# The FFN input products of a hybrid encoder by seven quarter products of fp32r pairs instead of eight

## The chip, the cores and the metric

The kernel runs on one core of one Trainium2 chip. The metric is the time of one execution on the device in microseconds (us). The engines are TensorE (PE in the profile, its weight loads PEld), VectorE (DVE), ScalarE (ACT), GpSimd (POOL) and SyncE (SP), which issues the DMAs.

## What is computed

Two layers of an encoder trunk on 512 tokens with 1024 features, in fp32:

```python
for i in range(DEPTH):                                   # DEPTH = 2
    h = h + 0.5 * swiglu_ffn(rms_norm(h, ffn1_norm[i]), ffn1_w_in[i], ffn1_w_out[i])
    u = rms_norm(h, mix_norm[i])
    z, xbc, dt_raw, q_a, kv_a, k_rope_raw = split_in_proj(u @ w_in_mix[i])
    y_ssd = ssd_mixer(...)                               # a chunked scan
    y_mla = mla_mixer(...)                               # latent attention, 8 heads
    h = h + jnp.concatenate([y_ssd, y_mla], axis=-1) @ w_out_mix[i]
    h = h + 0.5 * swiglu_ffn(rms_norm(h, ffn2_norm[i]), ffn2_w_in[i], ffn2_w_out[i])
    h = h + jax.nn.sigmoid(rms_norm(h, ple_norm[i]) @ w_ple_gate[i]) * (p[i] @ w_ple_proj[i])
return rms_norm(h, final_norm)

def swiglu_ffn(x, w_in, w_out):                          # w_in (1024, 5632), w_out (2816, 1024)
    g, u = jnp.split(x @ w_in, 2, axis=-1)
    return (jax.nn.silu(g) * u) @ w_out
```

There are four such FFNs, two in each layer. The change concerns the product `x @ w_in` in each of them.

## The kernel before

Activations lie transposed: features in the 128 partitions, the 512 tokens in the free dimension, so `h` is 8 tiles of 128x512. An fp32 product is made from three matmuls of fp32r, a type with a shorter mantissa: each operand is split into `hi`, its rounding to fp32r, and `lo`, the rest, and the product is hi x hi + hi x lo + lo x hi (`acc_wx`, lines 344 to 346), added up in a PSUM bank of 128x512.

Weights are planned as a list of units in the order in which the products take them. A unit is a tile `raw` of 128x1024 that one DMA loads (line 226); ScalarE rounds it to `hi` (L240) and VectorE subtracts to get `lo` (L241). `weights(key)` hands out the next unit and keeps the loads five units and the splits two units ahead (LOOK_DMA, LOOK_SPLIT); there are four raw tiles and three of `hi` and of `lo`.

An FFN (`ffn`) goes over 22 feature tiles f. For each, the gate's and the up-projection's product run over 8 tiles of the contraction, 24 matmuls of 512 columns each, into two banks. Then `evac` multiplies the gate by the token's norm factor `rb` (DVE, L465), applies SiLU (ACT, L467), multiplies by the up-projection (DVE, L468) and splits the result into `hi` and `lo` (`halves`, L357 on ACT and L358 on DVE). The output product then takes these 22 pairs as operands for each of 8 output tiles (66 matmuls each, with three weight units); the result is scaled (L500), added to `h` (L502), and the next norm gets the tile.

The norm's gain is multiplied into the operand while it is split (`add_operand`: ACT L382, DVE L383, two instructions of 512 columns for each of 8 tiles); the squares go into an accumulator (L404, L405), and the factor per token comes from it later (`stats`, `spread`).

The second FFN of a layer follows the mixer, whose last part adds the attention's output product to `h` tile by tile (L1088); the first FFN of the second layer follows the per-layer input (`ple`). In attention, `scores` makes the softmax rows of one block of 128 queries in a buffer `pr`, and `flip` transposes them, up to three blocks later.

Each `S()` takes one of 74 buffers of 128x512 (NSLOT), each `B()` one of eight PSUM banks. Between engines the framework sets the waits; it also sets the order in which each engine's instructions are issued: by the order of the code where two are ready, but one that is not ready is passed by later ones.

Of the kernel before, what the change touches and what calls it, by code (L numbers as in the profile page):

```python
# [17 lines left out]
P = 128  # L18
# [21 lines left out]
NSLOT = 74  # L40
NRAW = 4
NW = 3
LOOK_DMA = 5
LOOK_SPLIT = 2

# 2*pi as a sum of pieces; the first two have 12 bits, so that 11 bits times them are exact
# [20 lines left out]
class _Slots:  # L67
    """Buffers of one size, each with a tag of its own, handed out in the order they came free."""
# [17 lines left out]
def kernel(ctx: ExitStack, tc: tile.TileContext, a: dict, out: bass.AP):  # L86
# [8 lines left out]
    p_raw = ctx.enter_context(tc.tile_pool(name="p_raw", bufs=NRAW))  # L95
    p_hi = ctx.enter_context(tc.tile_pool(name="p_hi", bufs=NW))
# [10 lines left out]

    def sm(tag, shape, dt=F32, bufs=None):
        uid[0] += 1
        return small.tile(list(shape), dt, tag=tag, name=f"{tag}_{uid[0]}", bufs=bufs)  # L110
# [8 lines left out]
    units = []  # L119

    def unit(key, nk, cols, *loads):
        units.append((key, nk, cols, loads))
# [82 lines left out]
    loaded, split = [], []  # L205
    later = deque()

    def load_one():
# [3 lines left out]
        key, nk, cols, loads = units[len(loaded)]  # L212
# [14 lines left out]
        loaded.append((raw, nk, cols))  # L227
# [3 lines left out]

    def split_one():
        j = len(split)
        while len(loaded) <= j:
            load_one()
        raw, nk, cols = loaded[j]
# [3 lines left out]
        A.copy(hi[:, :n], raw[:, :n])  # L240
        V.tensor_tensor(lo[:, :n], raw[:, :n], hi[:, :n].bitcast(F32), op=ALU.subtract)  # L241
        loaded[j] = None
# [5 lines left out]
    def weights(key):  # L248
# [3 lines left out]
        while len(loaded) < min(j + 1 + LOOK_DMA, len(units)):  # L252
            load_one()
        while len(split) < min(j + 1 + LOOK_SPLIT, len(units)):
            split_one()
# [51 lines left out]
    tri = const.tile([P, P], F32, name="tri")        # 1 where row <= column  # L307
    stri = const.tile([P, P], F32, name="stri")      # 1 where row > column
# [6 lines left out]
    mk_l = const.tile([P, P], BF16, name="mk_l")     # row 0: queries of the first chunk  # L315
    mk_r = const.tile([P, P], BF16, name="mk_r")     # row 0: keys of the second chunk
# [44 lines left out]
    class Norm:  # L361
        """RMS norm over the feature tiles added to it: the gain goes into the products'
        operand, the per-token factor is applied to what the products give."""
# [26 lines left out]
        def add_part(self, y, src, cs):  # L390
            """Some columns of the last tile."""
# [6 lines left out]
        def add_square(self, src):  # L398
# [3 lines left out]
            else:  # L402
                sq = S()
                A.activation(sq.ap, src, AF.Square)  # L404
                V.tensor_tensor(self.acc.ap, self.acc.ap, sq.ap, op=ALU.add)  # L405
                slots.put(sq)
# [45 lines left out]

    def gain(i, nm):
        return lambda k: vcol(i, nm, k)
# [4 lines left out]
    def ffn(i, nm, norm, nxt, start=lambda: None, tables=lambda: None):  # L459
        hid = []  # L460

        def evac(bg, bu):
            # the per-token factor of `u` is applied after the output product
            g = S()
            V.tensor_tensor(g.ap, bg.ap, norm.rb.ap, op=ALU.mult)  # L465
            banks.put(bg)
            A.activation(g.ap, g.ap, AF.Silu)  # L467
            V.tensor_tensor(g.ap, bu.ap, g.ap, op=ALU.mult)  # L468
            banks.put(bu)
            hi, lo = S(F32R), S(F32R)  # L470
            halves(g.ap, hi.ap, lo.ap)
            slots.put(g)
            hid.append((hi, lo))

        X = norm.ops
        held = []
        for f in range(KF):
            bg, bu = B(), B()
            acc_wx(bg.ap, weights((i, nm, "g", f)), X)
            if f == 0:  # L480
                start()
                norm.stats()
            if f == 2:
                norm.spread()
            acc_wx(bu.ap, weights((i, nm, "u", f)), X)
            held.append((bg, bu))
            if f >= 2:
                for pair in held:
                    evac(*pair)
                held = []  # L490
            if f == 4:
                tables()
        norm.drop(rb=False)
        H = [(p.ap, q.ap) for p, q in hid]
        for m in range(KD):
            b = B()
            for k0 in range(0, KF, 8):
                acc_wx(b.ap, weights((i, nm, "o", m, k0)), H, k0, k0 == 0, k0 + 8 >= KF)
            t = S()
            V.scalar_tensor_tensor(out=t.ap, in0=b.ap, scalar=0.5, in1=norm.rb.ap, op0=ALU.mult, op1=ALU.mult)  # L500
# [812 lines left out]
```

## Time and profile before

| | |
|---|---|
| median of 3 runs | 2345.74 us (2345.72 to 2346.37) |
| span of the profiled execution | 2343.0 us (its own run time is not listed beside it) |
| TensorE busy | 2330.0 us, 10950 matmuls |
| VectorE busy | 1245.1 us, 1944 instructions |
| ScalarE busy | 885.3 us, 1388 instructions |
| GpSimd busy | 126.0 us, 136 instructions |
| mean granted TensorE clock | 0.999 of full speed |
| DMA | 209.73 MB, 90 GB/s in the mean |

The span runs from the first to the last instruction of the program. A row of a group gives the line, engine and operation, the written and read buffers, the shape, the count, and behind the bar the busy time in us, the mean of one in ns, and the engine's idle time just before these instructions with what ended it. A row of the timeline gives start and duration in us.

### The profile page before, as it was taken

The page shows a single profiled execution, that of the slowest core. Times are in us where ns is not written, and L with a number is a line of the kernel's source. Part 1 is how long each engine was busy: PE and PEld are TensorE (multiplying, and loading weights), DVE is VectorE, ACT ScalarE, POOL GpSimd, SP SyncE. Part 2 cuts the span into 40 slices and gives each one's busy share as a digit, 9 for nine tenths or more (in the row PEclk, how much of TensorE's full clock was granted, in tenths as well). Part 3 has the DMA queues.
Part 4 walks back from the last instruction along what each step waited for, and adds up shares of the span by engine and source line. Part 5 has one row for each costly group of instructions (what it writes and reads, how often), then busy time and mean ns, then how long its engine had stood idle before and what let it go on. Part 6 is the DMA issues. An engine that isn't in the chain of part 4 may idle for free.

```text
span 2343.0 us, 27624 instructions
## 1 busy us (share of the span) xinstructions
PE 2330.0 (99%) x10950; PEld 1933.4 (83%) x10950; DVE 1245.1 (53%) x1944; ACT 885.3 (38%) x1388; POOL 126.0 (5%) x136
## 2 busy tenths in 40 slices
PE   9999999999999999999999999999999999999998
PEld 7888888888888888888888888888888888888887
DVE  5543345688676434434644443466876764443345
ACT  4322224455455322222432222244544543222224
POOL 0000000223000000000000000011320000000000
PEclk9999999999999999999999999999999999999999
DMA  5333333221222333332333333332112223333322
GB/s 159 97 99 98 91 96 102 88 61 43 75 81 72 100 99 99 92 95 88 100 103 99 92 95 99 95 101 82 49 53 64 93 74 106 96 94 95 99 75 84
DMA packets 396110, 209.73 MB, mean 90 GB/s; under 512 B 19438, under 2 KB 390348, under 8 KB 395980
## 3 DMA queue, kind: packets, MB, share of 16 engines
q1 hardware_dynamic: 395980, 207.96, 30.6%
q8 instruction: 86, 1.41, 0.3%
q14 instruction: 44, 0.36, 0.0%
HBM read 205.83 MB, written 2.10 MB: 89 GB/s over the span
## 4 chain that ended last, share of the span: by engine, by line
PE 99%; DMA 0%; SPq 0%; DVE 0%; ACT 0%; POOL 0%; issue 0%
PE b L344 28%; PE b L345 28%; PE b L346 28%; PE b L353 2%; PE b L352 2%; PE b L354 2%; PE b L852 1%; PE b L1017 1%; PE b L1043 0%; PE b L833 0%; PE b L836 0%; PE b L993 0%; PE b L990 0%; PE b L1044 0%; PE b L992 0%; PE b L991 0%
## 5 line engine op out<-in xcount | busy, mean ns | idle before, releaser
L344 PE MATMUL b<-s,hi 128*128 128x512 f32 (+2 forms) x2906 | 1139.1, 393 | 0.0
L346 PE MATMUL b<-s,lo 128*128 128x512 f32 (+2 forms) x2906 | 1131.2, 390 | 0.0
L345 PE MATMUL b<-s,hi 128*128 128x512 f32 (+2 forms) x2906 | 1130.9, 390 | 0.0
L240 ACT CAST hi<-raw 128x1024 fp32r<-128x1024 f32 (+3 forms) x428 | 412.1, 963 | 1121.7 <-PE b L345 656.2
L241 DVE TENSOR_TENSOR lo<-raw,hi 128x1024 fp32r<-128x1024 f32 (+3 forms) x428 | 480.6, 1124 | 349.7 <-ACT hi L240 338.7
L346 PEld LDWEIGHTS b<-s,lo 128*128 128x128 f32 (+1 forms) x2906 | 545.4, 188 | 113.4
L344 PEld LDWEIGHTS b<-s,hi 128*128 128x128 f32 (+1 forms) x2906 | 545.8, 188 | 112.6 <-issue 2.4
L345 PEld LDWEIGHTS b<-s,hi 128*128 128x128 f32 (+1 forms) x2906 | 545.7, 188 | 112.5 <-issue 2.9
L468 DVE TENSOR_TENSOR s<-b,s 128x512 f32<-128x512 f32 x88 | 60.5, 691 | 254.6 <-PE b L346 250.9
L465 DVE TENSOR_TENSOR s<-b,s 128x512 f32<-128x512 f32 x88 | 60.1, 690 | 202.3 <-PE b L346 202.3
L430 POOL TENSOR_TENSOR nr<-nv,half 128x4 f32<-128x4 f32 (+1 forms) x14 | 19.1, 1366 | 1759.9 <-DVE nv L422 1759.1
L357 ACT CAST s<-b 128x128 fp32r<-128x128 f32 (+2 forms) x196 | 66.8, 360 | 102.6 <-DVE s L358 34.0
L358 DVE TENSOR_TENSOR s<-b,s 128x128 fp32r<-128x128 f32 (+2 forms) x196 | 75.4, 402 | 33.2 <-ACT s L357 31.7
L352 PE MATMUL b<-hi,s 128*128 128x512 f32 (+1 forms) x208 | 77.9, 375 | 0.0
L353 PE MATMUL b<-hi,s 128*128 128x512 f32 (+1 forms) x208 | 77.2, 371 | 0.0
L354 PE MATMUL b<-lo,s 128*128 128x512 f32 (+1 forms) x208 | 76.2, 366 | 0.0
L358 DVE TENSOR_TENSOR s<-s,s 128x512 fp32r<-128x512 f32 x104 | 71.0, 685 | 1.1 <-ACT s L357 0.7
L357 ACT CAST s<-s 128x512 fp32r<-128x512 f32 x104 | 64.6, 622 | 5.6 <-DVE s L976 4.6
L382 ACT ACTIVATE s<-s,vec 128x512 fp32r<-128x512 f32 x56 | 40.4, 722 | 56.4 <-DVE s L502 46.7
L608 DVE SCALAR_TENSOR_TENSOR s<-s,vec,s 128x511 f32<-128x511 f32 (+2 forms) x72 | 60.8, 848 | 0.6
L500 DVE SCALAR_TENSOR_TENSOR s<-b,s 128x512 f32<-128x512 f32 x32 | 22.1, 692 | 65.4 <-PE b L346 65.4
L467 ACT ACTIVATE s<-s 128x512 f32<-128x512 f32 x88 | 54.8, 626 | 0.4
(221 smaller groups left out, 1612.9 us busy)
## 6 DMA issues: line engine op xcount, KB each, us to landing
raw<-in_ffn_w_in_dram SPq DMA_DIRECT2D x176, 512.0 KB
raw<-in_ffn_w_out_dram SPq DMA_DIRECT2D x64, 512.0 KB
raw<-in_w_in_mix_dram SPq DMA_DIRECT2D x50, 512.0 KB
raw<-in_w_out_mix_dram SPq DMA_DIRECT2D x32, 512.0 KB
raw<-in_ffn_w_out_dram SPq DMA_DIRECT2D x32, 384.0 KB
raw<-in_w_ple_gate_dram SPq DMA_DIRECT2D x16, 512.0 KB
raw<-in_w_q_b_dram SPq DMA_DIRECT2D x16, 192.0 KB
s<-in_x_dram SPq DMA_DIRECT2D x8, 256.0 KB
```

Source lines behind the costliest of these rows:

```text
L240: A.copy(hi[:, :n], raw[:, :n])
L241: V.tensor_tensor(lo[:, :n], raw[:, :n], hi[:, :n].bitcast(F32), op=ALU.subtract)
L344: mm(b, lhsT=hi[:, kk, cs], rhs=xh, start=st, stop=False)
L345: mm(b, lhsT=hi[:, kk, cs], rhs=xl, start=False, stop=False)
L346: mm(b, lhsT=lo[:, kk, cs], rhs=xh, start=False, stop=en)
L352: mm(b, lhsT=xh[:, cs], rhs=hi[:, kk], start=first, stop=False)
L353: mm(b, lhsT=xl[:, cs], rhs=hi[:, kk], start=False, stop=False)
L354: mm(b, lhsT=xh[:, cs], rhs=lo[:, kk], start=False, stop=last)
L357: A.copy(hi, src)
L358: V.tensor_tensor(lo, src, hi.bitcast(F32), op=ALU.subtract)
L468: V.tensor_tensor(g.ap, bu.ap, g.ap, op=ALU.mult)
L608: V.scalar_tensor_tensor(out=y[:, s:], in0=x[:, :T - s], scalar=wc(3 - s), in1=y[:, s:], op0=ALU.mult, op1=ALU.add)
```

## The change

The product of the weights (taken as quarters: two halves of the contraction by two feature tiles) with the activations (two feature tiles of the contraction by two halves of 256 tokens) is a 2 x 2 block product. It takes eight quarter products; after the change seven, by Strassen's scheme in Winograd's form. The loop is over 11 pairs of feature tiles, j, for gate and up together.

- Weights: for each j four raw tiles 11, 21, 12, 22 (each with gate and up columns, 128x1024, two DMAs of 256 KB). Four sums of them are made on GpSimd into two new buffers `p_sum`: 11+12, that plus 22, that plus 21, and 12+22. The seven units (three raw tiles and four sums) are split as before. Five raw tiles instead of four; loads four raw tiles and sums three units ahead; 69 buffers instead of 74.
- Activations: `NormQ` takes the gained tiles in pairs, makes four combinations of their halves (three on DVE, one on GpSimd) and splits seven operands of 128x256 each.
- Products: each is 24 matmuls of 256 columns (gate and up in the two halves of one bank). Four banks per j; products 6, 7 and 3 add to a bank that an earlier product filled, after its earlier value was read.
- Evacuation: ScalarE copies three banks' values; four combinations on DVE join a bank with a copied or saved part; `gate` works on halves of 256 tokens. The split of the hidden tiles moves into the first output tile.
- Temporary buffers of the squares, of the output product's evacuation and of attention's `pr` come from the two `p_sum` buffers. The load of the per-layer input moves behind the last output product of the second FFN.

```diff
+NSLOT = 69
+NRAW = 5
+NSUM = 2
+LOOK_DMA = 4
+LOOK_SUM = 3
...
     def plan_ffn(i, nm, w_in, w_out):
-        for f in range(KF):
-            unit((i, nm, "g", f), KD, P, (None, kview(w_in, 0, KD, f * P, P)))
-            unit((i, nm, "u", f), KD, P, (None, kview(w_in, 0, KD, FF + f * P, P)))
+        wq = w_in.rearrange("(k two p) f -> two p k f", two=2, p=P)
+        for j in range(KF // 2):
+            r = {}
+            for b, (kh, f) in (("11", (0, 2 * j)), ("21", (1, 2 * j)), ("12", (0, 2 * j + 1)), ("22", (1, 2 * j + 1))):
+                r[b] = ("raw", raw(4, 256, (slice(0, P), wq[kh, :, :, f * P:(f + 1) * P]),
+                                   (slice(P, 2 * P), wq[kh, :, :, FF + f * P:FF + (f + 1) * P])))
+            n = len(units)
+            for p, src, more in ((1, r["11"], None), (2, r["21"], None), (5, r["11"], r["12"]),
+                                 (6, ("sum", n + 2), r["22"]), (4, ("sum", n + 3), r["21"]),
+                                 (7, r["12"], r["22"]), (3, r["22"], None)):
+                units.append(((i, nm, j, p), 4, 256, src, more))
...
+    def sum_one():
...
+        if more is not None:
+            t = p_sum.tile([P, 1024], F32, tag="sum", name=f"sum{j}")
+            G.tensor_tensor(t, source(src), source(more), op=ALU.add)
+            sums[j] = t
...
+    class NormQ(Norm):
...
+        def quarters(self, e, o):
+            a11, a21, a12, a22 = e[:, :HT], e[:, HT:], o[:, :HT], o[:, HT:]
+            s, t = S(), S()
+            s1, s2, s3, s4 = s[:, :HT], s[:, HT:], t[:, :HT], t[:, HT:]
+            V.tensor_tensor(s1, a21, a22, op=ALU.subtract)
+            V.tensor_tensor(s2, s1, a11, op=ALU.subtract)
+            G.tensor_tensor(s3, a11, a21, op=ALU.subtract)
+            V.tensor_tensor(s4, a12, s2, op=ALU.add)
+            for p, x in ((1, a11), (2, a12), (5, s1), (6, s2), (4, a22), (7, s3), (3, s4)):
+                y = S(F32R)
+                halves(x, y[:, :HT], y[:, HT:])
+                self.O[p].append(y)
+            slots.put(s, t)
...
+        def product(bank, j, p, first):
+            hi, lo = weights((i, nm, j, p))
+            ops = norm.O[p]
+            for gu in range(2):
+                o = bank[:, gu * HT:(gu + 1) * HT]
+                cs = slice(gu * P, (gu + 1) * P)
+                for k in range(4):
+                    x = ops[k]
+                    mm(o, lhsT=hi[:, k, cs], rhs=x[:, :HT], start=first and gu == k == 0, ...)
+                    mm(o, lhsT=hi[:, k, cs], rhs=x[:, HT:], ...)
+                    mm(o, lhsT=lo[:, k, cs], rhs=x[:, :HT], ...)
+        def gate(c, h, a):
+            ts = slice(a * HT, (a + 1) * HT)
+            V.tensor_tensor(c[:, :HT], c[:, :HT], norm.rb[:, ts], op=ALU.mult)
+            A.activation(c[:, :HT], c[:, :HT], AF.Silu)
+            V.tensor_tensor(h[:, ts], c[:, :HT], c[:, HT:], op=ALU.mult)
+        for j in range(NJ):
+            product(ba, j, 1, True);   A.copy(s1.ap, ba.ap)
+            product(bc, j, 2, True);   V.tensor_tensor(c11.ap, bc.ap, s1.ap, op=ALU.add)
+            product(bb, j, 5, True)
+            product(ba, j, 6, False);  A.copy(s2.ap, ba.ap);  gate(c11, h0, 0)
+            product(bd, j, 4, True)
+            product(ba, j, 7, False);  A.copy(u3.ap, ba.ap)
+            V.tensor_tensor(c22.ap, bb.ap, u3.ap, op=ALU.subtract)
+            V.tensor_tensor(c21.ap, bd.ap, u3.ap, op=ALU.add)
+            product(bb, j, 3, False);  gate(c22, h1, 1);  gate(c21, h0, 1)
+            V.tensor_tensor(c12.ap, bb.ap, s2.ap, op=ALU.subtract);  gate(c12, h1, 0)
...
+                if m == 0:
+                    for x in hid[k0:k0 + nk]:
+                        hi, lo = S(F32R), S(F32R)
+                        halves(x.ap, hi.ap, lo.ap)
...
-            pr = S()
+            pr = tmp()
```

The loop over j is shortened here: buffer handling is left out and several statements stand on one line.

More of the change, by code (lines that the diff above doesn't have):

```diff
@@ L106, with tmp @@
     uid = [0]
+    def tmp():
+        uid[0] += 1
+        return p_sum.tile([P, 1024], F32, tag="sum", name=f"tmp{uid[0]}")[:, :T]
     def sm(tag, shape, dt=F32, bufs=None):
@@ L203 @@
         plan_layer(i)
-    loaded, split = [], []
+    loaded, sums, split = [], {}, []
     later = deque()
@@ L239, in split_one @@
         lo = p_lo.tile([P, 1024], F32R, tag="lo", name=f"lo{j}")
[L240 to L242 removed]
+        A.copy(hi[:, :n], x[:, :n])
+        V.tensor_tensor(lo[:, :n], x[:, :n], hi[:, :n].bitcast(F32), op=ALU.subtract)
         split.append((hi[:, :n].rearrange("p (k f) -> p k f", k=nk),
@@ L251, in weights @@
         taken[0] += 1
-        while len(loaded) < min(j + 1 + LOOK_DMA, len(units)):
+        for n in range(j, min(j + 1 + LOOK_SUM, len(units))):
+            fetch(n)
+        while len(loaded) < len(raws) and len(loaded) < last_raw[j] + 1 + LOOK_DMA:
             load_one()
+        while summed[0] < min(j + 1 + LOOK_SUM, len(units)):
+            sum_one()
         while len(split) < min(j + 1 + LOOK_SPLIT, len(units)):
@@ L257, in weights @@
         return got
+    last_raw = []
+    for u in units:
+        top = max([x[1] for x in u[3:] if x is not None and x[0] == "raw"], default=-1)
+        last_raw.append(max(top, last_raw[-1] if last_raw else -1))
     ident = const.tile([P, P], F32, name="ident")
@@ L456, with ffn @@
     h = []
-    def ffn(i, nm, norm, nxt, start=lambda: None, tables=lambda: None):
+    def ffn(i, nm, norm, nxt, start=lambda: None, tables=lambda: None, between=lambda: None):
         hid = []
[L462 to L480, printed above, removed]
+        NJ = KF // 2
+        def product(bank, j, p, first):
[6 more added lines that the diff above has]
+                    x = ops[k]
+                    mm(o, lhsT=hi[:, k, cs], rhs=x[:, :HT], start=first and gu == k == 0, stop=False, skip_group_check=not first)
+                    mm(o, lhsT=hi[:, k, cs], rhs=x[:, HT:], start=False, stop=False, skip_group_check=not first)
+                    mm(o, lhsT=lo[:, k, cs], rhs=x[:, :HT], start=False, stop=gu == 1 and k == 3, skip_group_check=not first)
+            if j == NJ - 1:
+                norm.drop_product(p)
+        def gate(c, h, a):
[3 more added lines that the diff above has]
+            V.tensor_tensor(h[:, ts], c[:, :HT], c[:, HT:], op=ALU.mult)
+            slots.put(c)
+        for j in range(NJ):
+            h0, h1 = S(), S()
+            hid += [h0, h1]
+            ba, bc = B(), B()
+            product(ba, j, 1, True)
+            s1 = S()
+            A.copy(s1.ap, ba.ap)
+            product(bc, j, 2, True)
+            if j == 0:
@@ L481, in ffn @@
                 start()
                 norm.stats()
-            if f == 2:
-                norm.spread()
[L485 to L491, printed above, removed]
+            c11 = S()
+            V.tensor_tensor(c11.ap, bc.ap, s1.ap, op=ALU.add)
+            banks.put(bc)
+            slots.put(s1)
+            bb = B()
```

116 lines of the change are left out of this document (88 added, 28 removed).

## Prediction

> **What bounds the kernel now.** I read the page first: the span, the busy time of each engine, and the chain of work that ended last.
>
> ```profile
> span 2343.0 us, 27624 instructions
> PE 2330.0 (99%) x10950; PEld 1933.4 (83%) x10950; DVE 1245.1 (53%) x1944; ACT 885.3 (38%) x1388; POOL 126.0 (5%) x136
> PE 99%; DMA 0%; SPq 0%; DVE 0%; ACT 0%; POOL 0%; issue 0%
> ```
>
> TensorE is busy from end to end and is the whole chain, so whatever shortens its stream shortens the kernel, as long as nobody makes it wait. VectorE is about half used, GpSimd hardly at all. Then the view of stretches, for the FFN input products of the first layer and for the moment at which the second FFN starts:
>
> ```profile
> 60.00:250.00 190.00, 190.00 (x840) 157.15 (x839) 83.10 (x113) 56.38 (x74) 0.00 (x0) 1.00 0.33 95
> 738.00:760.00 22.00, 22.00 (x102) 18.33 (x101) 13.25 (x19) 12.44 (x19) 0.00 (x0) 1.00 0.26 77
> 760.00:765.00 5.00, 5.00 (x24) 4.14 (x23) 4.96 (x8) 1.24 (x2) 0.00 (x0) 1.00 0.61 179
> ```
>
> The columns are length, then busy time and count of PE, weight loads, DVE, ACT and POOL, then clock, DMA share and GB/s. In the input products 840 matmuls take 190 us: one each 0.226 us. (The mean of a matmul on the page, 0.39 us, is its latency; matmuls overlap, so starts must be used.) DVE fills 44% of that stretch and DMA a third. At the start of an FFN (last row) DVE is full.
>
> **The matmuls.** For each j (two feature tiles of gate and up) the kernel before issues 2 x 2 x 8 x 3 = 96 matmuls of 512 columns: 96 x 0.226 = 21.7 us. After, 7 products x 2 x 4 x 3 = 168 matmuls of 256 columns, each with its own weight load. That is 7/8 of the columns, but is a 256-column matmul half of a 512-column one? The last tile of the kernel before has 60 in a row, with the same weight loads; first and last in the timeline, behind the last wide one:
>
> ```profile
> 2323.60 0.39 PE L346 MATMUL b<-s,lo 128*128 128x512 f32 x1
> 2323.83 0.28 PE L344 MATMUL b<-s,hi 128*128 128x256 f32 x1
> ...
> 2330.90 0.28 PE L346 MATMUL b<-s,lo 128*128 128x256 f32 x1
> ```
>
> 59 steps in 7.07 us: 0.120 us each, 53% of 0.226. So 168 x 0.120 = 20.1 us. The work removed from TensorE is 1.6 us per j, not the 2.7 us that an eighth would be; with 11 j in each of 4 FFNs, 44 x 1.6 = 70 us. This is all that can be gained; the rest is what eats it.
>
> **VectorE and GpSimd in the loop.** Durations, from the groups of instructions with shapes kept apart and from the timeline (a row with x2 or x3 is that many, back to back):
>
> ```profile
> L241 DVE TENSOR_TENSOR lo<-raw,hi 128x1024 fp32r<-128x1024 f32 x342 | 422.2, 1235 | 322.3 <-ACT hi L240 311.5
> L468 DVE TENSOR_TENSOR s<-b,s 128x512 f32<-128x512 f32 x88 | 60.5, 691 | 254.6 <-PE b L346 250.9 <-PE b L329 3.4
> L358 DVE TENSOR_TENSOR s<-b,s 128x256 fp32r<-128x256 f32 x16 | 6.7, 419 | 1.6 <-ACT s L357 1.6
> L240 ACT CAST hi<-raw 128x1024 fp32r<-128x1024 f32 x342 | 359.2, 1051 | 946.9 <-PE b L345 538.5 <-issue 383.8 <-PE b L353 22.8
> L357 ACT CAST s<-b 128x256 fp32r<-128x256 f32 x16 | 6.1, 379 | 6.5 <-DVE s L358 6.5
> L442 ACT COPY s<-b 128x512 f32<-128x512 f32 x10 | 5.8, 581 | 4.6 <-PE b L440 4.6
> ```
>
> ```profile
> 29.49 2.34 DVE L241 TENSOR_TENSOR lo<-raw,hi 128x1024 fp32r<-128x1024 f32 x2
> 45.19 1.88 DVE L465 TENSOR_TENSOR s<-b,s 128x512 f32<-128x512 f32 x3
> 45.91 1.83 ACT L467 ACTIVATE s<-s 128x512 f32<-128x512 f32 x3
> 46.99 1.28 DVE L468 TENSOR_TENSOR s<-b,s 128x512 f32<-128x512 f32 x2
> ```
>
> Back to back, DVE starts a 1024-column instruction each 2.34 - 1.22 = 1.12 us, a 512-column one each (1.88 - 0.69) / 2 = 0.60; for 256 columns I take 0.42 - 0.09 = 0.33. After, each j has seven weight splits instead of four, four combinations of a bank with a saved part (512), and eight gate multiplications (256): 7 x 1.12 + 4 x 0.60 + 8 x 0.33 = 12.9 us of DVE. ScalarE has 7 x 1.05 + 3 x 0.58 + 4 x 0.38 = 10.6 us, which lies beside. The four sums on GpSimd are 128x1024 with two dense operands. No such row exists; the nearest are the shortest of two narrower forms:
>
> ```profile
> 501.22 1.27 POOL L804 TENSOR_TENSOR s<-s,s 128x512 f32<-128x512 f32 x1 [1.23 <-DVE s L802]
> 572.07 0.46 POOL L561 TENSOR_TENSOR s<-s,s 128x128 f32<-128x128 f32 x1 [2.56 <-DVE s L560]
> ```
>
> 0.81 us for 384 columns is 2.1 ns per column, so 1.27 + 512 x 2.1 ns = 2.35 us (from a fixed cost alone, 1.27, to proportional, 2.54). Four are 9.4 us of POOL per j. Alone this fits in 20.1 us easily. But the mixer's rows show that the two engines exclude each other:
>
> ```profile
> 498.96 1.04 POOL L773 TENSOR_TENSOR s<-tri,d_dAl 128x512 fp32r<-128x512 f32 x1
> 499.02 1.52 DVE L820 SCALAR_TENSOR_TENSOR s<-s,y_r,s 128x512 f32<-128x512 f32 x1 [0.44 <-POOL y_r L815]
> 549.49 0.74 DVE L820 SCALAR_TENSOR_TENSOR s<-s,y_r,s 128x512 f32<-128x512 f32 x1
> 502.56 1.55 POOL L773 TENSOR_TENSOR s<-tri,d_dAl 128x512 fp32r<-128x512 f32 x1
> 503.13 2.06 DVE L241 TENSOR_TENSOR lo<-raw,hi 128x1024 fp32r<-128x1024 f32 x1
> 523.39 0.68 DVE L756 TENSOR_TENSOR s<-b,d_skip 128x512 f32<-128x512 f32 x1
> 523.62 2.17 POOL L763 TENSOR_TENSOR s<-s,d_dec 128x512 f32<-128x512 f32 x2 [0.85 <-DVE s L755]
> ```
>
> L820 reads two buffers of SBUF and takes 0.74 us alone (549.49); started 0.06 us behind a POOL instruction (498.96 to 500.00) it ends 0.54 us after that one: it waited for all of it. The weight split L241 does the same at 503.13: it ends 1.08 us behind POOL's 504.11. The other way, POOL's 1.04 grows to 1.55 behind a DVE instruction. L756, with one operand in a PSUM bank, keeps its 0.68 beside the POOL work that starts at 523.62. A switch gives some overlap back (0.74 - 0.54 = 0.20; 1.22 - 1.08 = 0.14). In the loop the splits and gate multiplications read two SBUF buffers, the four combinations don't. So DVE and POOL together need 12.9 + 9.4 - 4 x 0.17 = 21.6 us per j if no combination falls beside a sum, and 21.6 - 2.4 = 19.2 us if all four do. TensorE needs 20.1. The loop then is a contest between two full resources. I take 21.6: DVE works in order, a blocked split holds the combination behind it, and there are only three split buffers, so a sum in front of a split (2.35 + 1.05 + 1.12 of the two products' 5.8 us) uses up most of the lead. The loop's gain: 44 x (21.7 - 21.6) = 4 us, from 44 x 1.6 = 70 us if TensorE sets the pace.
>
> The Trainium skill (SBUF — State Buffer, "Who interferes with whom") states the rule that speaks against this change: a DVE instruction with two SBUF inputs and a GpSimd instruction that reads SBUF fully block each other for the whole instruction. By the letter of it, without the 0.17 given back, the loop's bounds would be 22.3 and 19.9 us, some 30 us more over 44 j. The rows above give a little less than a whole block, and I go by them.
>
> **The wait before the third product.** Product 3 adds into the bank that product 5 filled and that DVE must first read, with a part that ScalarE copies out after product 7: at least 0.58 + 0.69 us behind the matmul that ended last, 44 times 1.3 = 56 us if TensorE stood. I cost it at nothing, because the order of issue isn't that of the code: at 45.19 DVE does three of L465 before the first L468, though the code has L465, L468 pair by pair. Product 1 of the next j has its own bank, and its weights are split two products ahead, so it can go in front. If it does not, 20.1 + 1.3 = 21.4 us, about the same loop.
>
> **What each FFN adds at its edges.**
>
> ```profile
> L383 DVE SCALAR_TENSOR_TENSOR s<-s,vec,s 128x512 fp32r<-128x512 f32 x56 | 41.9, 749 | 24.1 <-ACT s L382 24.1
> L382 ACT ACTIVATE s<-s,vec 128x512 fp32r<-128x512 f32 x56 | 40.4, 722 | 56.4 <-DVE s L502 46.7 <-DVE s L1171 8.2 <-DVE s L1088 1.5
> L358 DVE TENSOR_TENSOR s<-s,s 128x512 fp32r<-128x512 f32 x104 | 71.0, 685 | 1.1 <-ACT s L357 0.7
> L357 ACT CAST s<-s 128x512 fp32r<-128x512 f32 x104 | 64.6, 622 | 5.6 <-DVE s L976 4.6 <-DVE s L468 0.3
> ```
>
> Start: for two feature tiles, two L383 (0.66 apart) give way to three sums and seven splits of 256 columns: 10 x 0.33 - 1.3 = 2.0 us more DVE, and 7 x 0.38 = 2.7 us more ACT; four pairs add 8 and 11 us. DVE is already full when the second FFN starts (760 to 765). TensorE can run the first three pairs' parts of three products meanwhile (54 x 0.12 = 6.5 us). Between nothing and 11 us for each FFN, 5 taken: 20 us for four.
>
> Output products: the 22 hidden tiles were split in the loop; now the first output tile does it, 22 x 0.60 = 13.2 us of DVE with three weight splits (3.4) beside 66 x 0.226 = 14.9 us of TensorE: 1.7 us short, and up to 3.2 us before the first (combination 0.69, gate 0.42 + 0.38 + 0.42, split 0.62 + 0.69, one behind the other). Between nothing, where DVE's gaps take some earlier, and 5: 4 taken, 16 us.
>
> Attention's probabilities now share two buffers where they could hold three. A block's exponential waits for the transposes two blocks before; with 64 blocks and dense products to fill in, between nothing and 64 x 0.58 (the copy of one bank) = 37 us: 4 taken, since TensorE has other work there. Weight traffic is the same in bytes, a third of DMA's time before: nothing. None of these edges can gain, as TensorE waited for none of them.
>
> **Sum.** 2343.0 - 4 + 20 + 16 + 4 = 2379 us of span; the median of the runs, 2345.74, lies 2.7 above the profiled span, so 2382 us.
>
> **Rivals.** First, faster: TensorE sets the pace. The combinations fall beside the sums and DVE's need is 19.2 us; the loop takes 20.1 and the edges cost 30: 2345.7 - 70 + 30 = 2306. For it speaks that the bound is below 20.1; against it, that two resources would both have to be full all the time. It decides at 20.8 us per j, where 40 us of edges are paid. Chance 0.27. Second, slower still: DVE rarely runs back to back, because each step waits for ScalarE, TensorE or a sum. Then full durations count: 7 x 1.235 + 4 x 0.69 + 8 x 0.42 + 9.4 = 24.2 us per j, 44 x 2.5 = 110 us: 2345.7 + 110 + 40 = 2496; half way to it, 2440. In the window from 60 DVE waits more than it works, which speaks for it; that full DVE runs back to back (45.19) against. Chance 0.18. Third, the split doesn't do what it says because narrow matmuls stay bound by weight loads: the 60 in a row at 0.120 speak against; at 0.129 and more nothing is left to gain, which gives 2386 with the edges, in the forecast's range. Chance 0.03.
>
> **Numbers.** Forecast 0.52, faster rival 0.27, slower rival 0.18, weight loads 0.03. A difference of 0.2% (4.7 us) is what can be told from none. The faster rival and a part of the forecast's low end give faster 0.28; 20.7 to 20.9 us per j gives same 0.06; the rest slower 0.66. The range takes in the faster rival and half of the slower one: 2300 to 2450; the forecast's own is 2350 to 2420.
>
> **What would show it.** In the profile after: matmuls of 256 columns 0.120 us apart inside a product; j periods of 21 to 22 us with TensorE idle before a product and released by a weight split on DVE; POOL sums near 2.35 us, longer when behind DVE; splits of 2 us and more beside them; a pause at the start of each FFN. Wrong if DVE has gaps while TensorE is full, or if the splits keep 1.2 us beside the sums.

## The result, and the profile after

The changed kernel takes 2501.81 us (median of 4 runs, 2500.16 to 2503.45) where the kernel before takes 2345.73 (2345.70 to 2346.37): a ratio of 1.0665, 95% interval 1.065 to 1.068. It is 156 us slower. That is on the forecast's side, but 120 us above the forecast's 2382, beyond its range, and 6 us above the second rival's 2496.

The page of the kernel after, its span, its busy times and its chain of work:

```profile
span 2501.0 us, 36116 instructions
PE 2328.8 (93%) x14118; PEld 2061.9 (82%) x14118; DVE 1893.4 (76%) x2556; ACT 1123.4 (45%) x1852; POOL 630.0 (25%) x328
PE 72%; DVE 20%; ACT 3%; issue 2%; POOL 2%; DMA 1%; DVEq 0%; SPq 0%; POOLq 0%; ACTq 0%
```

TensorE was the whole chain before; now a fifth of the chain is VectorE. The stretches: one j of the first FFN, then nine j's and the start of the second FFN (length, then busy time and count of PE, weight loads, DVE, ACT, POOL, then clock, DMA share, GB/s):

```profile
126.92:150.37 23.45, 20.92 (x170) 20.31 (x169) 22.05 (x20) 9.96 (x15) 10.71 (x5) 1.00 0.31 91
846.00:1056.00 210.00, 187.99 (x1505) 182.51 (x1503) 195.88 (x169) 88.85 (x125) 97.27 (x36) 1.00 0.31 90
800.00:812.00 12.00, 6.12 (x23) 4.46 (x21) 12.00 (x29) 10.53 (x28) 2.94 (x3) 0.65 0.00 0
812.00:824.00 12.00, 8.53 (x42) 8.12 (x43) 8.66 (x21) 4.02 (x8) 7.08 (x1) 0.64 0.16 45
824.00:836.00 12.00, 9.13 (x50) 8.79 (x49) 5.59 (x6) 5.30 (x7) 9.13 (x4) 0.71 0.15 44
```

A j takes 23.45 us, where the kernel before takes 96 x 0.226 = 21.7 and the forecast said 21.6. TensorE idles 23.45 - 20.92 = 2.53 us of it. Most j's have this length to 0.01 us; it is a locked rhythm. In the last three rows TensorE is busy half to three quarters of the time, at a granted clock of 0.64 to 0.71. Now one j in the timeline: start, duration, and in brackets the engine's idle time before it with its releaser.

```profile
147.39 5.69 DVE L286 TENSOR_TENSOR lo<-raw,hi 128x1024 fp32r<-128x1024 f32 x3
147.52 0.39 PE L567 MATMUL b<-s,lo 128*128 128x256 f32 x1 [0.89 <-DVE lo L286]
147.60 3.26 POOL L273 TENSOR_TENSOR sum<-sum,raw 128x1024 f32<-128x1024 f32 x1 [1.55 <-DVE lo L286]
152.00 0.38 PE L567 MATMUL b<-s,lo 128*128 128x256 f32 x1 [1.35 <-DVE lo L286]
...
154.86 1.05 ACT L285 CAST hi<-sum 128x1024 fp32r<-128x1024 f32 x1 [2.99 <-PE b L566]
155.94 1.22 DVE L286 TENSOR_TENSOR lo<-sum,hi 128x1024 fp32r<-128x1024 f32 x1 [0.99 <-ACT hi L285]
157.08 2.96 DVE L576 TENSOR_TENSOR s<-s 128x256 f32<-128x256 f32 x2
157.29 2.47 POOL L273 TENSOR_TENSOR sum<-sum,raw 128x1024 f32<-128x1024 f32 x1 [6.43 <-DVE lo L286]
160.45 0.69 DVE L618 TENSOR_TENSOR s<-b,s 128x512 f32<-128x512 f32 x1 [0.41 <-PE b L567]
163.35 2.45 POOL L273 TENSOR_TENSOR sum<-raw,raw 128x1024 f32<-128x1024 f32 x1 [3.59 <-DVE lo L286]
166.94 0.39 PE L567 MATMUL b<-s,lo 128*128 128x256 f32 x1 [0.29 <-DVE lo L286]
166.97 2.52 POOL L273 TENSOR_TENSOR sum<-raw,raw 128x1024 f32<-128x1024 f32 x1 [1.16 <-DVE lo L286]
170.96 0.39 PE L567 MATMUL b<-s,lo 128*128 128x256 f32 x1 [0.89 <-DVE lo L286]
```

Read 147.39 and 152.00 together. Three weight splits, 1.12 us each when back to back, take 5.69: 2.2 more than 2 x 1.12 + 1.22 = 3.46. The sum that starts at 147.60 and ends at 150.86 lies in that time. The third matmul of a product is the first that needs `lo`; it waits for the blocked split until 152.00. A j has three such waits, 1.35 + 0.29 + 0.89 = 2.53 us, which is all of TensorE's idle time; each also costs the refill of the matmul pipeline (a matmul behind a wait lasts 0.39, the steady step is 0.12). So 23.45 - 2.53 - 3 x 0.27 = 20.1: without the waits the j would have the predicted 168 x 0.120. DVE in turn stands idle twice, 0.99 + 0.41 = 1.40 us: for a `hi` whose cast TensorE releases late, and for a bank that TensorE fills late.

The groups, shapes kept apart (count | busy us, mean ns | idle before, releaser):

```profile
L286 DVE TENSOR_TENSOR lo<-raw,hi 128x1024 fp32r<-128x1024 f32 x298 | 447.2, 1519 | 214.4 <-ACT hi L285 213.9
L286 DVE TENSOR_TENSOR lo<-sum,hi 128x1024 fp32r<-128x1024 f32 x176 | 291.2, 1656 | 45.7 <-ACT hi L285 45.7
L576 DVE TENSOR_TENSOR s<-s 128x256 f32<-128x256 f32 x176 | 236.5, 1375 | 1.0 <-ACT s L575 1.0
L618 DVE TENSOR_TENSOR s<-b,s 128x512 f32<-128x512 f32 x44 | 30.3, 690 | 16.2 <-PE b L567 16.2
L273 POOL TENSOR_TENSOR sum<-sum,raw 128x1024 f32<-128x1024 f32 x88 | 253.2, 2878 | 344.2 <-DVE lo L286 310.9 <-DVE s L459 13.4 <-DMA raw<-in_ffn_w_in_dram 8.3
L273 POOL TENSOR_TENSOR sum<-raw,raw 128x1024 f32<-128x1024 f32 x88 | 232.7, 2646 | 222.0 <-DVE lo L286 119.3 <-DMA raw<-in_ffn_w_in_dram 66.8 <-DVE s L459 30.2
```

What reads two SBUF buffers on DVE has grown: splits from 1235 ns to 1519 and 1656, the gate multiplication L576 to 1375 where 0.42 us was taken. The combination L618 with one operand in a PSUM bank keeps its 690 (691 before). A sum takes 2.45 alone; the mean is higher because it waits inside the instruction too.

Where the 158 us of span went, by stages (us against the kernel before; an FFN's stages end where DVE has scaled their last output tile, L500 before, a mixer with its last addition to `h`; "input" is an FFN from its start through its first output tile):

| | FFN 1a input | FFN 2a input | FFN 1b input | FFN 2b input | outputs, each of 4 | mixers, each of 2 |
|---|---|---|---|---|---|---|
| before, us | 272.1 | 252.2 | 253.3 | 252.2 | 104.7 | 383.4 (first) |
| after | +45.5 | +47.8 | +29.0 | +44.9 | -4.5 | +3.8, +4.0 |
| without sums (e3) | -0.2 | +2.7 | -6.5 | +2.0 | -6.3 | +3.8, +3.8 |
| sums on DVE (e1) | +10.0 | +8.3 | -3.4 | +7.3 | -4.5 to -6.8 | +3.8, +3.7 |

The minus at the outputs is no gain. TensorE needs 14.96 us for an output tile before and after; the second tile ends only 10.43 us after the first (8.61 in e3), so part of it ran before the first one's end, and that time lies under "input".

Counting all 44 j at the common length, the loops are 44 x (23.45 - 21.72) = 76 us of it, the mixers 8, and what is left, the edges of the FFNs, 74.

### The profile page after: what moved, and what is told of

Same layout as the page of the kernel before. It is cut to its first block, busy times and chain, and to the rows that moved or that the text cites. A ratio compares the mean times of both kernels' runs of the same rounds, so it can differ in the third digit from the quotient of the medians.

```text
span 2501.0 us, 36116 instructions
## 1 busy us (share of the span) xinstructions
PE 2328.8 (93%) x14118; PEld 2061.9 (82%) x14118; DVE 1893.4 (76%) x2556; ACT 1123.4 (45%) x1852; POOL 630.0 (25%) x328
## 4 chain that ended last, share of the span: by engine, by line
PE 72%; DVE 20%; ACT 3%; issue 2%; POOL 2%; DMA 1%; DVEq 0%; SPq 0%; POOLq 0%; ACTq 0%
PE b L398 13%; PE b L400 13%; PE b L399 13%; DVE lo L286 12%; PE b L567 9%; PE b L565 7%; PE b L566 7%; PE b L407 1%; PE b L406 1%; PE b L408 1%; POOL sum L273 1%; DVE s L574 1%; DVE s L618 1%; DVE s L591 1%; DVE s L576 1%
## 5 line engine op out<-in xcount | busy, mean ns | idle before, releaser
L567 PE MATMUL b<-s,lo 128*128 128x256 f32 x2464 | 720.5, 293 | 120.8 <-DVE lo L286 120.8
L566 PE MATMUL b<-s,hi 128*128 128x256 f32 x2464 | 707.7, 289 | 13.0 <-DVE s L412 13.0
L565 PE MATMUL b<-s,hi 128*128 128x256 f32 x2464 | 702.8, 288 | 12.2 <-ACT hi L285 8.2
L286 DVE TENSOR_TENSOR lo<-raw,hi 128x1024 fp32r<-128x1024 f32 (+3 forms) x384 | 510.5, 1344 | 246.7 <-ACT hi L285 246.2
L567 PEld LDWEIGHTS b<-s,lo 128*128 128x128 f32 x2464 | 484.5, 197 | 146.5 <-DVE lo L286 146.4
L398 PE MATMUL b<-s,hi 128*128 128x512 f32 (+1 forms) x1498 | 590.9, 397 | 2.0 <-ACT tmp L1142 2.0
L400 PE MATMUL b<-s,lo 128*128 128x512 f32 (+1 forms) x1498 | 583.0, 390 | 3.7 <-DVE lo L286 3.7
L399 PE MATMUL b<-s,hi 128*128 128x512 f32 (+1 forms) x1498 | 581.5, 389 | 0.0
L566 PEld LDWEIGHTS b<-s,hi 128*128 128x128 f32 x2464 | 484.6, 197 | 16.5 <-DVE s L412 16.2
L565 PEld LDWEIGHTS b<-s,hi 128*128 128x128 f32 x2464 | 482.1, 197 | 14.8 <-ACT hi L285 9.4
L273 POOL TENSOR_TENSOR sum<-sum,raw 128x1024 f32<-128x1024 f32 x88 | 253.2, 2878 | 344.2 <-DVE lo L286 310.9
L400 PEld LDWEIGHTS b<-s,lo 128*128 128x128 f32 x1498 | 280.8, 187 | 64.7 <-DVE lo L286 6.3
L398 PEld LDWEIGHTS b<-s,hi 128*128 128x128 f32 x1498 | 281.2, 188 | 59.7 <-ACT tmp L1142 2.7
L399 PEld LDWEIGHTS b<-s,hi 128*128 128x128 f32 x1498 | 281.1, 188 | 57.8 <-issue 2.9
L286 DVE TENSOR_TENSOR lo<-sum,hi 128x1024 fp32r<-128x1024 f32 x176 | 291.2, 1656 | 45.7 <-ACT hi L285 45.7
L273 POOL TENSOR_TENSOR sum<-raw,raw 128x1024 f32<-128x1024 f32 x88 | 232.7, 2646 | 222.0 <-DVE lo L286 119.3
L576 DVE TENSOR_TENSOR s<-s 128x256 f32<-128x256 f32 x176 | 236.5, 1375 | 1.0 <-ACT s L575 1.0
```

Source lines behind the costliest of these rows:

```text
L273: G.tensor_tensor(t, source(src), source(more), op=ALU.add)
L286: V.tensor_tensor(lo[:, :n], x[:, :n], hi[:, :n].bitcast(F32), op=ALU.subtract)
L398: mm(b, lhsT=hi[:, kk, cs], rhs=xh, start=st, stop=False)
L399: mm(b, lhsT=hi[:, kk, cs], rhs=xl, start=False, stop=False)
L400: mm(b, lhsT=lo[:, kk, cs], rhs=xh, start=False, stop=en)
L565: mm(o, lhsT=hi[:, k, cs], rhs=x[:, :HT], start=first and gu == k == 0, stop=False, skip_group_check=not first)
```

## The experiments

The theory after the result: DVE's weight split and GpSimd's sum exclude each other, and a sum that gets in front of a split that TensorE already waits for stops TensorE (theory 1). The rivals: the sums themselves come late, whatever they exclude (theory 2); the two engines' work together is more than a j holds, the prediction's capacity view; and, for the starts, that the sums queue behind the buffers of the squares, against DVE simply having too much to do.

### e1: the sums on DVE

```diff
-            G.tensor_tensor(t, source(src), source(more), op=ALU.add)
+            V.tensor_tensor(t, source(src), source(more), op=ALU.add)
```

> The four sums of weight quarters are made on VectorE instead of GpSimd, nothing else. In the changed kernel a j takes 23.45 us (the same stall at 126.92 and at 150.37), VectorE is busy for 22.05 of them. Theory 1, the two engines block each other: without GpSimd's sums VectorE needs 12.9 + 4 x 1.12 = 17.4 us per j, less than TensorE's 20.1, so the loop falls to 20.1 to 20.8 us and the whole from 2502 by 44 x 2.6 to 3.3 us to 2356 to 2386. Theory 2, the sums come late because of their own length and of the two buffers they share: VectorE takes over 4.5 us of work in a chain that stays, the loop gains at most the 1.2 us by which a sum is shorter, four times at most once per j: 2450 or more. A third view, VectorE was full by its own work: the loop gets longer, over 2502.

2353.32 us (median of 6, 2351.5 to 2355.37), ratio 1.003 (1.0017 to 1.0042): 148 of the 156 us are gone with one letter, slightly better than theory 1 put it. A stretch of the second FFN's loop, and groups:

```profile
805.00:990.00 185.00, 182.83 (x1516) 182.05 (x1516) 162.21 (x209) 92.09 (x130) 0.00 (x0) 1.00 0.36 103
```

```profile
L286 DVE TENSOR_TENSOR lo<-sum,hi 128x1024 fp32r<-128x1024 f32 x176 | 214.0, 1217 | 5.4 <-ACT hi L285 5.4
L273 DVE TENSOR_TENSOR sum<-sum,raw 128x1024 f32<-128x1024 f32 x88 | 107.3, 1220 | 15.9 <-DMA raw<-in_ffn_w_in_dram 15.3
```

Most j's take 20.2 to 20.4 us. DVE makes a sum in 1.22 us, GpSimd in 2.45. (The Trainium skill, GPSIMD Engine Reference, "4.1 Engine selection", gives two-input elementwise work to VectorE, GpSimd being about twice as slow; these two numbers agree.) DVE, now with all of the work, is busy 88% of the stretch, where it was 93% with less to do: much of that was waiting inside instructions.

### e2: GpSimd writes the buffers, and reads eight columns

The sums are left out: two fills of the buffer take about as long, and an addition of the first 8 columns keeps the waits.

```diff
-            G.tensor_tensor(t, source(src), source(more), op=ALU.add)
+            G.memset(t, 1.0)
+            G.memset(t, 1.0)
+            G.tensor_tensor(t[:, :8], source(src)[:, :8], source(more)[:, :8], op=ALU.add)
```

> Each sum on GpSimd is replaced by two fills of the whole sum buffer and an addition of its first 8 columns: GpSimd works about as long in the same place, waits for the same raw tiles and writes the same buffer, but hardly reads SBUF. The sums themselves are left out, so the products of four of the seven units are of constants. Theory 1 (blocking through reads): splits and gate multiplications return to 1.22 and 0.42 us, the loop to 20.1 to 20.5 us, 2350 to 2375 in all. Theory 2 (sums late by their length): the loop stays within 0.5 us of 23.45 and the whole over 2470.

2350.54 us (one run). Groups and a stretch of the loop:

```profile
L274 POOL MEMSET sum<- 128x1024 f32 x176 | 168.0, 955 | 7.8
L288 DVE TENSOR_TENSOR lo<-sum,hi 128x1024 fp32r<-128x1024 f32 x176 | 214.5, 1219 | 114.3 <-ACT hi L287 114.2
```

```profile
800.00:1000.00 200.00, 199.91 (x1647) 197.88 (x1647) 135.09 (x197) 103.89 (x151) 79.36 (x114) 1.00 0.35 100
```

GpSimd is nearly as busy beside the splits as it is with sums (40% of the stretch; 46% after); it holds a buffer for 79.36 / 38 = 2.1 us, not much less than a sum, and a j takes 20.41. So it is not the sums' length or lateness (theory 2 falls) but their reading of SBUF. The Trainium skill (SBUF — State Buffer, "Who interferes with whom") says that a DVE instruction with two SBUF inputs contends with a GpSimd instruction that reads SBUF and not with one that only writes it: this run agrees, with 1219 ns for the split beside fills and 1656 beside sums.

### e3: no sums at all

The four units of a sum split their second raw tile alone; the sums are left out.

```diff
-            t = p_sum.tile([P, 1024], F32, tag="sum", name=f"sum{j}")
-            G.tensor_tensor(t, source(src), source(more), op=ALU.add)
-            sums[j] = t
+            sums[j] = source(more)
```

> No sums at all: the four units that were sums split the second raw tile alone, so that part of the computation is left out. This is the bound of what any other place for the sums can give. VectorE needs 12.9 us per j. Both theories: the loop at TensorE's 20.1 to 20.3 us, and the starts of the FFNs without a wait for the first sum. Theory 1 has this equal to the write-only run within 20 us; theory 2 has it 100 us below that run. About 2340 to 2365; what then stays above 2345.7 - 70 = 2276 is the price of the edges.

2324.72 us (one run), below what was expected, and 26 us below e2, where theory 1 had put the two within 20 us and theory 2 100 us apart. A stretch of the loop, and the first j of the second FFN:

```profile
770.00:980.00 210.00, 210.00 (x1745) 210.00 (x1745) 142.80 (x207) 109.30 (x157) 1.01 (x1) 1.00 0.35 101
752.97:787.36 34.39, 28.41 (x182) 26.25 (x181) 28.91 (x59) 23.37 (x46) 3.24 (x3) 0.80 0.23 68
```

In the loop TensorE is full, and a j takes 20.16 us: the seven narrow products, their combinations and the wait before product 3 all run at TensorE's pace. The change without its sums takes 20 us less of span than the kernel before: 44 x (20.16 - 21.72) = -69, +8 in the mixers, and so +41 at the edges. These lie in the first j of each FFN: 31.96, 34.39, 25.13 and 33.69 us, together 44.5 more than four times 20.16. From the last j to the end of the outputs TensorE waits once in each FFN, for 0.98 us. The step from here to the kernel after, 178 us of span, is the price of GpSimd's sums: 44 x (23.45 - 20.16) = 145 in the loops, 33 more at the edges.

### e8 and e11: how many sums, and how long each

e8 puts the two sums of two raw tiles on DVE and leaves two on GpSimd; e11 cuts every sum on GpSimd into two instructions.

```diff
-            G.tensor_tensor(t, source(src), source(more), op=ALU.add)
+            (V if src[0] == "raw" else G).tensor_tensor(t, source(src), source(more), op=ALU.add)
```

```diff
-            G.tensor_tensor(t, source(src), source(more), op=ALU.add)
+            for c in (slice(0, 512), slice(512, 1024)):
+                G.tensor_tensor(t[:, c], source(src)[:, c], source(more)[:, c], op=ALU.add)
```

> The changed kernel with two of the four sums (11+12 and 12+22) on VectorE, the other two on GpSimd. VectorE and GpSimd together need 12.9 + 2 x 1.12 + 2 x 2.35 - 0.3 = 19.5 us per j, under TensorE's 20.1, if they block each other and both are used without pause; all four on GpSimd needed 21.6 by the same sum and took 23.45, 1.8 more. If that 1.8 us is a fixed loss (one engine waiting while the other holds the ports, split buffers), the loop is 21.0 to 21.5, the whole 2502 - 44 x 2.2 = 2400 to 2410 or less by a few us at the starts; if it comes per sum, half of it and the bound is passed: 20.2 to 20.6, 2360 to 2380.

> The changed kernel with each GpSimd sum in two instructions of 512 columns, same work. In the run with two sums on GpSimd VectorE and GpSimd had room (19.5 us of need, 2 us of idle time on VectorE) and the loop still took 22.0 us: three pauses of 0.5, 1.0 and 1.5 us per j with four sums, one of 1.5 with two, each while a weight split stood behind a sum. If it is the length of one sum that delays the split that is due, halves let the split in between: the loop falls from 23.45 to 21.8 to 22.6 us, the whole to 2430 to 2465. If the two engines' total bounds it, the halves add 4 x 0.1 to 0.2 us of fixed cost per j: 23.4 to 24.0, 2500 to 2525.

e8: 2424.12 us (one run), above both expectations. Most j's take 22.0, a few 20.4. The stretch, and the timeline around a sum (of a j of 20.4) and a pause (of a j of 22.0):

```profile
850.00:1030.00 180.00, 170.81 (x1392) 167.56 (x1391) 163.95 (x181) 87.48 (x126) 42.29 (x16) 1.00 0.34 97
```

```profile
903.20 3.38 POOL L273 TENSOR_TENSOR sum<-sum,raw 128x1024 f32<-128x1024 f32 x1 [10.93 <-DVE lo L286]
923.22 2.64 POOL L273 TENSOR_TENSOR sum<-sum,raw 128x1024 f32<-128x1024 f32 x1 [9.97 <-DMA raw<-in_ffn_w_in_dram]
927.00 0.39 PE L567 MATMUL b<-s,lo 128*128 128x256 f32 x1 [1.34 <-DVE lo L286]
```

A j of 22.0 has exactly one pause, 1.34 to 1.35 us plus the refill, and the j with the sum at 903.20 has none: the same work per j, otherwise timed. DVE is idle 9% of the stretch, and by the starts and ends of their rows one of DVE and GpSimd runs for 19.9 us of a mean j of 21.6, less than TensorE's 20.16. Here the two don't have too much to do, and TensorE waits all the same.

e11: 2461.39 us (one run), inside its expectation. The group, the stretch, one j of it, and that j's two pauses before a `lo` (a third, 0.20 us, ends with a copy of ScalarE):

```profile
L274 POOL TENSOR_TENSOR sum<-sum,raw 128x512 f32<-128x512 f32 x176 | 309.8, 1780 | 246.0 <-issue 183.6 <-DVE lo L287 44.2 <-DMA raw<-in_ffn_w_in_dram 12.1
```

```profile
860.00:1050.00 190.00, 178.14 (x1434) 173.07 (x1433) 173.38 (x167) 87.45 (x128) 113.28 (x68) 1.00 0.32 92
881.58:903.89 22.31, 20.94 (x171) 20.33 (x170) 20.23 (x21) 9.86 (x14) 13.62 (x8) 1.00 0.34 97
```

```profile
897.78 0.39 PE L568 MATMUL b<-s,lo 128*128 128x256 f32 x1 [0.94 <-DVE lo L287]
901.15 0.38 PE L568 MATMUL b<-s,lo 128*128 128x256 f32 x1 [0.23 <-DVE lo L287]
```

Almost every j takes 22.31 us, 1.14 less, with the same columns added on GpSimd and more instructions to do it (113.28 us busy in 190, against 97.27 in 210 of the kernel after). If the two engines' work filled the j, this could only have made it longer, so it doesn't fill it: in the kernel after one of DVE and GpSimd runs for 22.04 us of a j and neither for 1.41; in e11 it is 21.97 and 0.34. What the halves take away is time in which both stand still. The capacity view falls as the period of the loop, but not as a floor: the common time is 22.0 us with halves as without, 1.9 above TensorE's 20.16, and e11 lies just above it.

### e4, e5, e9 and e12: the starts

e4 takes the squares out of the sums' two buffers into buffers of their own (the sums stay on GpSimd). e9 is e1 with that. e5 is e1 with the operands of products 1, 2 and 5 made first and the other four after the last tile. e12 is e9 with e5's order.

```diff
-                sq = tmp()
+                sq = S()
...
+                slots.put(sq)
```

> The squares of the norms get buffers of their own again instead of the two that the sums use; all else as changed, sums on GpSimd. At the second FFN's start the first sum waited until 811 for a square and the second until 824. If this sharing makes the slow starts, the four starts gain 4 to 8 us each and the whole falls to 2470 to 2485, the loop staying at 23.4 us. If the starts are slow because VectorE and ScalarE are full with the seven operands' splits, nothing changes: 2497 to 2505.

> Sums on VectorE, and at an FFN's start only the operands of products 1, 2 and 5 are made tile by tile; those of 6, 4, 7 and 3 of all four pairs follow behind the last tile, their one difference on VectorE too instead of GpSimd. Same work, other order. With the sums on VectorE the second FFN's start still shows pauses of 1 to 2.4 us between 763 and 775 and the clock at 0.6 to 0.7. Theory A, the start is late because the first products' operands queue behind all seven splits of the earlier pairs: six or seven of ten of these DVE steps (4 pairs x 7 x 0.33 = 9 us) leave the way, the two second FFNs gain 6 to 9 us each and the first 3 to 6, 2330 to 2340 in all. Theory B, the start is bound by the sum of VectorE's work whatever its order: 2348 to 2356 as with the sums on VectorE alone (2353).

> Sums on VectorE and the squares in buffers of their own; five raw tiles and the two shared buffers for sums and attention as in the changed kernel. On GpSimd's sums the squares' own buffers gained 7 us at each second FFN. If that gain was the wait of the sums for a square's buffer, it is there with VectorE's sums as well, 2 to 4 us each, and 2353 falls to 2345 to 2349; if it was GpSimd's starving alone, 2352 to 2356.

> As the run with VectorE's sums and the squares' own buffers, with the operands of the first three products made first. The order alone gained nothing (2357 against 2353), the three-buffer runs differed by 1 us. 0 to 4 us below or above the other, 2342 to 2352; the kernel before is at 2345.7, so no difference that can be told from it.

| | us | against 2345.6 to 2345.8 |
|---|---|---|
| e4 | 2487.19 (one run) | 14.6 less than after |
| e5 | 2357.26 (one run) | e1 is 2353.32 |
| e9 | 2355.22 (median of 4, 2350.36 to 2358.23) | ratio 1.0043 (1.0027 to 1.006) |
| e12 | 2353.12 (median of 5, 2352.61 to 2354.86) | ratio 1.0033 (1.002 to 1.0046) |

e4 lies between its two expectations. Its loop keeps its 23.45 us; its gain is at the starts of the second FFNs (8.7 and 5.6 us). What it takes away is seen in the kernel after, at 811.29, and what comes in its place in e4:

```profile
811.29 7.79 POOL L273 TENSOR_TENSOR sum<-raw,raw 128x1024 f32<-128x1024 f32 x1 [6.27 <-DVE s L459]
812.47 2.09 DVE L412 TENSOR_TENSOR s<-s,s 128x256 fp32r<-128x256 f32 x6
824.01 2.44 POOL L273 TENSOR_TENSOR sum<-sum,raw 128x1024 f32<-128x1024 f32 x1 [4.94 <-DVE s L459]
```

```profile
801.47 0.97 POOL L534 TENSOR_TENSOR s<-s 128x256 f32<-128x256 f32 x1 [2.91 <-ACT s L520]
805.26 11.16 POOL L534 TENSOR_TENSOR s<-s 128x256 f32<-128x256 f32 x1 [2.83 <-ACT s L520]
```

In the first, the sum waited 6.27 us for the squares (L459 frees their buffer) and then ran 7.79 us instead of 2.45, beside DVE instructions that follow one another without a gap up to 816.84. In the second, a quarter operand of 128x256 on GpSimd takes 11.16 us at the same point. With the sums on DVE none of this helps: e5, e9 and e12 stay within 4 us of e1 (e5 1 us above its theory B, e9 as with GpSimd's starving alone, e12 1 us above its range). So, of the two theories of the starts, the buffers cost only where GpSimd makes the sums. That the rest is the amount of DVE's and ACT's work is argued, not shown: the one other order that was tried shortened nothing, and no run takes the work away.

### e6 and e7: three sum buffers, four raw tiles

e6 is e9 with a third sum buffer, paid for with a raw tile; e7 adds e5's order.

```diff
-NRAW = 5
-NSUM = 2
+NRAW = 4
+NSUM = 3
```

> Sums on VectorE; three instead of two of the shared buffers (one raw tile less), so attention's rows have three again, and the squares have buffers of their own. Each mixer took 383.4 us before and 387.2 in every changed kernel so far. If the two shared buffers of attention are the cause, the mixers return to 383 to 384 each, 7 us in all; if not, 387. The squares' own buffers: up to 3 us per second FFN. Together 2353 falls to 2338 to 2346; 2350 or more if four raw tiles make the loads late.

> Sums on VectorE, first products' operands first, three shared buffers and the squares in their own: all edits together. If the edges' causes are told rightly their gains add: 2353 - 13 to 20 (starts) - 7 (mixers) = 2326 to 2333, under the kernel before (2345.8) by 0.5% to 0.8%. If the start is bound by VectorE's sum of work, 2343 to 2349, no difference from before. The floor is the run without any sums, 2324.7, less what these edits save there as well.

Both missed: 2382.83 us (median of 4, 2380.83 to 2383.43), ratio 1.0157 (1.014 to 1.0174), and 2381.96 (median of 4, 2381.22 to 2382.09), ratio 1.0154 (1.0139 to 1.0169). In three FFNs most j's run at 20.16 us, steadier than in e1, but in one of them at 21.5 (in e6 the third FFN, in e7 the second). There, in e6:

```profile
1350.65 2.48 DVE L273 TENSOR_TENSOR sum<-sum,raw 128x1024 f32<-128x1024 f32 x2 [1.10 <-DMA raw<-in_ffn_w_in_dram]
1354.33 0.39 PE L568 MATMUL b<-s,lo 128*128 128x256 f32 x1 [1.04 <-DVE lo L286]
```

A sum waits for a load, and the split that follows on DVE comes late. By this row four raw tiles are one too few; no run changes the raw tiles alone. From the last j to the end of the outputs an FFN takes 147.3 to 149.1 us, and 142.3 in e9: TensorE waits there for 4.2 to 5.3 us instead of 1.3. The third buffer gives little to the mixers: they are 2.4 us longer than before in e6, where e9 has 3.3, and 1.4 in e7, where e12 has 2.1. Three buffers with five raw tiles would need space taken elsewhere; it wasn't tried.

### e10: the kernel before, with attention's rows in two buffers

The changed kernel's loss in the mixers has nothing to do with sums (e3 has it too). Here the kernel before gets the change's restriction alone.

```diff
-            pr = S()
+            pr = p_pr.tile([P, T], F32, tag="pr", name="pr")
```

`p_pr` has two buffers, and NSLOT is 73.

> The kernel before with one part of the change alone: attention's rows in two buffers that they rotate through, instead of one of the 74 each time (73 left). Each mixer took 383.4 us before and 387.2 after. If the two buffers cost it, the mixers take 386 to 388 here and the whole 2350 to 2354; if not, 383 to 384 and 2345 to 2347, and the mixers' loss is in the order of the raw tiles' loads or in the fewer buffers.

2350.45 us (one run), and +2.0 us in each mixer: half of the 3.8 to 4.0. For the mixers that lies between the two expectations. For the other half e5 and e12 give a hint: with four of the seven operands put behind the last tile the mixers are 2.5 and 2.1 us longer than before instead of 3.8 (e1) and 3.3 (e9), so some of it is the next norm's splits in front of the mixer's last additions. The smaller number of buffers (69) and the other weight order before and after are candidates that were not tried.

## Why the prediction was wrong, step by step

**The matmuls: right.** 168 x 0.120 = 20.1 us; with nothing in the way a j took 20.16 (e3), and 44 j's gained 69 us, 70 predicted.

**The prices of the operations: right.** Splits of 1.22 us, 0.42 for a gate, 0.69 for a combination that the sums don't touch (690 ns), 2.45 for a sum where 2.35 was worked out, and the exclusion of the two engines, read from the mixer's rows: in the kernel after each sum holds DVE up by 2.2 us, and, as assumed, no combination falls beside a sum (153.00, 153.60, 160.45 and 161.06 all lie between them).

**The loop's 21.6 us: the step that failed.** The prediction made from these prices a sum of busy time, 12.9 + 9.4 - 0.7, and took the larger of this need and TensorE's 20.1 as the period. The need was right: one j of the kernel after has 13.4 us of DVE's own work (13.38 in e3), 8.7 more in which sums hold it up, and so DVE is busy for 22.05 us, 0.4 more than 21.6. Wrong was to take this floor for the period, with no time in which DVE stands idle: it is idle for 1.40 us of each j (155.94 and 160.45), and GpSimd with it.

That the need isn't all is shown by e11, with the same columns to add, more instructions and a j 1.14 us shorter, and by e8, where the two engines' time fits under TensorE's and a j still takes 22.0 instead of 20.16. What comes on top of the need is latency at one place: a split that TensorE needs now, behind a sum that has just begun; TensorE's pause then comes back to DVE, which waits for the `hi` and the bank that TensorE gives late. The prediction had seen the piece, a sum in front of a split uses up most of the lead, and put no price on it. So of the 23.45 - 20.16 = 3.3 us that four sums cost per j, 1.9 are the need above TensorE's pace and 1.4 the idle time. The sum by this step is 80 of the 122 us that were missed of the span: 44 x 1.73 = +76 instead of -4; 44 x 1.40 = 62 of it is the idle time that the prediction had put at nothing.

Why does a sum get in at just this moment? The rows of the sums name it: they are released by `lo` of L286. A sum starts when a split has read the buffer that it will overwrite or the lead count has advanced, that is at a split's end, when DVE's next split is due. That this timing is the cause of the locked rhythm was read from the rows, not tried.

**The edges: near without the sums by luck, wrong with them.** 36 us were predicted, 20 at the starts and 16 at the output products. Without the sums (e3) 41 are measured, but as 44.5 in the first j's and one wait of 0.98 us per FFN behind them: the starts were put at half of what they cost, the output products at four times, and the two errors nearly cancel. In the kernel after it is 74. The 33 more are what the prediction left out: it priced DVE's and ACT's added work, but not that the sums, on an engine that DVE's back-to-back run shuts out, would arrive last (7.79 us for one). Nor did it price the clock: the mean granted clock is 0.983 of a span of 2501.0 us, and since the trace grants either 1.00 or 0.50 (0.50 from 804 to 817, for instance), this is (1 - 0.983) / 0.5 x 2501 = 85 us at half speed. The kernel before has 2.7, at its very end, where TensorE has nothing left to do. Without the sums it is 46 us (0.990 of 2323.0), so a part of e3's edges is the clock's too. At most half of these times is lost to the clock; how much, beside the waits that bring it about, stays open.

**The wait before product 3: right at nothing** (e3, TensorE busy 210.00 of 210.00 us). **Attention: right at 4 us** for the two buffers (2 x 2.0 in e10); the mixers lost 8, and the other 4 were in no term.

**The rivals.** The first, TensorE setting the pace, is what happens without GpSimd's reads: 20.3 to 20.4 us in e1, 20.41 in e2; there the loop's gain of some 58 us is eaten by edges, sums and mixers, and ends 8 us above the kernel before. The second came within 6 us of the time, by luck: it had 110 us for the loop, where 76 are measured, and 40 for the edges, where it is 82 with the mixers. Its reason, that full durations count because DVE rarely runs back to back, isn't what the trace shows: DVE does run back to back (behind the three splits of 147.39 the two combinations start at 153.00 and 153.60, 0.60 apart), and without reads on GpSimd the same instructions fit in 20.4 us (e2). The third, weight loads, is excluded by 20.16.

**What the Trainium skill's rule would have given** (SBUF — State Buffer, "Who interferes with whom", a full block): 22.3 us per j as the bound in total. Measured are 22.05 us in which DVE is busy or held up, and 23.45 in all. The rule is borne out as to who blocks whom; the 1.40 us above them aren't a matter of how much of the block is given back.

No version here that computes everything beats the kernel before. The best are e1 and e12, 2353 us, 0.3% slower.

## What to carry to other kernels

When two engines exclude each other, the total of their busy times is a floor for the loop, not its period. Price on top of it the longest instruction of the one against the lead of the other at the place where the bound engine waits; cutting the side engine's instructions in halves, with the same work to do, gave back 1.14 of the 3.29 us per j. Put an addition that feeds a critical chain on the engine of that chain, even at 88% of its time, before giving it to an idle engine that shares its reading. And when a scheme saves an eighth of the work in one stage, add up its edges (41 us here, of 69 gained) before anything else: without any sums at all, this one would have gained 0.9%.

## What was not expected of the hardware

- DVE instructions without a gap between them can shut GpSimd out for long: 11.16 us for an instruction that takes 0.74 to 0.97, 7.79 for one of 2.45.
- GpSimd's fills of 128x1024 (955 ns) beside the same splits cost the splits nothing (1219 ns).
- At the start of an FFN where TensorE was busy 51 to 76% of the time, with waits of 0.3 to 2.3 us one behind the other and none longer, the granted clock was down to 0.64 to 0.71 in the mean for 36 us.
